# A one-layer streaming encoder on eight cores: from a hand-ordered kernel to an operation graph list-scheduled over three overlapped token tiles

## The chip, the cores and the metric

The kernel runs on all 8 cores of one Trainium2 chip: two dies of four cores. Every core does the same work on 4 of the 32 sequences. The time is device microseconds (us) of the slowest core. Engines are named as in the profile: PE is TensorE, PEld its weight loads, DVE is VectorE, ACT is ScalarE, POOL is GpSimd, SP is the queue that issues the DMAs. PSUM is the memory into which PE writes, used by both kernels as eight banks (`ps` of eight after; `psA` of six and `psT` of two before); an eviction is the DVE or ACT operation that reads a bank out.

The 8-core runs show two states. In the fast one the cores of a kernel agree within 1% (one run of before, 1.2%); in the slow one cores of one die, or of both, show a lower granted TensorE clock. **Only fast runs are compared below** unless a sentence says otherwise.

## The reference, cut to what matters

```python
D_MODEL = 1024; BATCH = 32; SEQ = 2048; DEPTH = 1; CHUNK = 64; D_FF = 4096; PLE_DIM = 256
def reference(x, p, ...):
    h = rmsnorm(x, g_mix)
    q, k, v, g, u, sv = split(h @ w_in)                  # 6 x 512 columns
    r = layernorm_nogain(chunk_retention(rotary(q), rotary(k) * 128**-0.5, v)) * ret_norm_g
    y_ret = silu(g) * r                                  # retention, 4 heads of 128
    y_sg = spatial_gating(gelu(u), gelu(sv), w_s, b_s, sg_norm_g)
    x = x + concat([y_ret, y_sg]) @ w_out                # "mixer"
    x = x + square(relu(rmsnorm(x, g_ffn) @ w_ff1)) @ w_ff2      # "FFN"
    x = x + sigmoid(rmsnorm(x, g_ple) @ w_ple_gate) * (p @ w_ple)   # "gate"
    return rmsnorm(x, g_final)
```

Inputs and output are float32; both kernels multiply in bfloat16. A core has 8192 tokens, worked through in 16 tiles of 512. Only the retention state ties one tile to the next.

## The kernel before

A small helper records operations per engine in the order in which the Python calls them, and works out semaphore waits. Each engine's program is its list, in that order. Per tile the order is written by hand: four 128-token blocks (`b`) are staggered by one or two steps in the mixer, then comes the FFN, then the gate.

```python
def norm_elem(b, xs_):                         # every norm: square-sum, rstd, scale
    S.add("act", ... activation(out=xsb[:, b, :], in_=xb[:, xs_, :], func=AF.Square, accum_out=stats...))
    rstd_from_ss(...)                          # DVE (mult, add), ACT Sqrt, DVE reciprocal
    S.add("act", ... activation(out=xsb[:, b, :], in_=xb[:, xs_, :], func=AF.Identity, scale=rstd))

def norm_transpose(b, gcol):                   # 8 PE transposes, then DVE eviction with the gain
    for kc in range(8): S.add("pe", ... transpose(out=psT[...], in_=xsb[:, b, ...]))
    S.add("dve", ... tensor_tensor(out=actT[...], in0=psT[...], in1=gT[...], op=ALU.mult))
# [cut]
norm_transpose(0, 0); norm_transpose(1, 0); stage_X1(0); stage_X1(1)
norm_transpose(2, 0); norm_transpose(3, 0); phase_B()
order = [("X2", 0), ("X2", 1), ("Y", 0), ("X", 2), ("Y", 1), ("Z", 0), ("X", 3), ("Y", 2), ("Z", 1),
         ("W", 0), ("Y", 3), ("Z", 2), ("W", 1), ("DT", 0), ("Z", 3), ("W", 2), ("DT", 1), ("W", 3),
         ("DT", 2), ("DT", 3)]
for nm, b in order: fns[nm](b)

for u in range(8):                             # FFN, first half: weights stream through a ring of 3
    slot = next_unit()
    for f4 in range(4):
        f = u * 4 + f4
        # 8 matmuls 128x512 into one PSUM bank
        S.add("act", ... Relu: psA -> scr)
        S.add("dve" if f % 2 == 0 else "pool", ... square: scr -> hT)
# [cut] second half: 32 matmuls into each of 4 banks, then a DVE add into the residual
# [cut] gate: norm_transpose, 8+2 matmuls, ACT Sigmoid, DVE multiply, POOL add, final norm, store
```

Activations use Silu, Gelu_apprx_tanh, Sigmoid and Sqrt. `w_in`'s v, g, u and sv columns, `w_out` and `w_ple_gate` stay in SBUF; q, k and the FFN weights stream. The float32 weights are cast to bfloat16 by DMAs on the POOL queue at the start.

Of the kernel before, what the change touches and what calls it, by code (L numbers as in the profile page):

```python
# [6 lines left out]
F32 = mybir.dt.float32  # L7
BF16 = mybir.dt.bfloat16
I32 = mybir.dt.int32
# [8 lines left out]
NRING = 3  # L18
N_CORES = 8
SEQ_PER_CORE = 4  # L20

class Op:
    __slots__ = ("eng", "fn", "dma", "ndma", "key", "val", "marked", "waits", "clock", "rank")

class Sched:
    ENGS = ("pe", "act", "dve", "pool", "sp")

    def __init__(self):
        self.eng_ops = {e: [] for e in self.ENGS}
        self.comp_ops = {e: [] for e in self.ENGS}  # L30
        self.issue_clock = {e: {} for e in self.ENGS}
        self.last_writer = {}
        self.readers = {}
        self.dma_cum = {}
        self.n_ops = 0

    def add(self, eng, fn, reads=(), writes=(), dma=None, ndma=1):
        op = Op()
        op.eng, op.fn, op.dma, op.ndma = eng, fn, dma, ndma
        op.marked = False  # L40
        self.eng_ops[eng].append(op)
        self.n_ops += 1
        if dma is None:
            self.comp_ops[eng].append(op)
            op.key, op.val = eng, len(self.comp_ops[eng])
        else:
            cum = self.dma_cum.get(dma, 0) + 16 * ndma
            self.dma_cum[dma] = cum
            op.key, op.val = ("dma", dma), cum
        deps = []  # L50
        for b in reads:
            w = self.last_writer.get(b)
            if w is not None:
                deps.append((w, 0))
        for b in writes:
            w = self.last_writer.get(b)
            if w is not None:
                deps.append((w, 1))
            for r in self.readers.get(b, {}).values():
                deps.append((r, 2))  # L60
        clk = self.issue_clock[eng]
        waits = {}
        for d, kind in deps:
            if d is op:
                continue
            if d.dma is None and d.eng == eng and dma is None:
                if eng == "pe" or kind != 0:
                    continue
# [8 lines left out]
        op.waits = list(waits.items())  # L77
        op.clock = dict(clk)
        op.clock[op.key] = op.val
        for b in reads:  # L80
            self.readers.setdefault(b, {})[op.key] = op
        for b in writes:
            self.last_writer[b] = op
            self.readers[b] = {}
        return op
# [9 lines left out]
def _emit_engine(eng_name, eobj, sched, sems):  # L95
    comp = sched.comp_ops
    for op in sched.eng_ops[eng_name]:
# [6 lines left out]
        if op.dma is not None:  # L104
            if not isinstance(ins, (list, tuple)):
                ins = [ins]
            assert len(ins) == op.ndma
            for i_ in ins:
                i_.then_inc(sems[op.key], 16)
        elif op.marked:  # L110
            ins.then_inc(sems[op.key], 1)

def _host_consts():
# [5 lines left out]
    ci = (t // 64)[:, None]  # L119
# [23 lines left out]
    ROT = np.zeros((SEQ // TT, 128, 2, TT), f32)  # L143
    for tp in range(SEQ // TT):
# [7 lines left out]

def build(nseq):
    NT = nseq * (SEQ // TT)
    NTOK = NT * TT
    nc = bass.Bass("TRN2", target_bir_lowering=False)
# [5 lines left out]
    p_d = din("p", [NTOK, 256])  # L162
    w_in_d = din("w_in", [D, 3072])
    w_out_d = din("w_out", [D, D])
    w1_d = din("w_ff1", [D, 4096])
    w2_d = din("w_ff2", [4096, D])
    wg_d = din("w_gate", [D, D])
    wple_d = din("w_ple", [256, D])
# [10 lines left out]
    ROT_d = din("ROT", [SEQ // TT, 128, 2, TT])  # L179
    IDENT_d = din("IDENT", [128, 128])  # L180
    out_d = nc.dram_tensor("out", [NTOK, D], F32, kind="ExternalOutput").ap()
    wqkb_d = nc.dram_tensor("wqkb", [2, 128, 4096], BF16, kind="Internal").ap()
    w1b_d = nc.dram_tensor("w1b", [8, 128, 4096], BF16, kind="Internal").ap()
    w2b_d = nc.dram_tensor("w2b", [8, 128, 4096], BF16, kind="Internal").ap()

    S = Sched()
# [5 lines left out]
    with es:  # L192
        win = sb("win", [128, 8, 2048], BF16)
        wout = sb("wout", [128, 8, 1024], BF16)
        wgs = sb("wgs", [128, 8, 1024], BF16)
        wple = sb("wple", [128, 2, 1024], BF16)
        ring = sb("ring", [128, NRING, 8, 512], BF16)
        xb = sb("xb", [128, 6, D], F32)
        actT = sb("actT", [128, 8, TT], BF16)
        big = sb("big", [128, 16384], BF16)  # L200
        rot = sb("rot", [128, 2, TT], F32)
        pbf = sb("pbf", [128, NB, 256], BF16)
        pT = sb("pT", [128, 2, TT], BF16)
        scr = sb("scr", [128, 4, 1024], F32)
        xsb = sb("xsb", [128, NB, D], BF16)
        Sst = sb("Sst", [128, 512], F32)
        Sbf = sb("Sbf", [128, 2, 512], BF16)
# [3 lines left out]
        retg = sb("retg_s", [128, 512], F32)  # L211
        sgg = sb("sgg_s", [128, 512], F32)
        bsT = sb("bsT_s", [128, 4], F32)
        wsTf = sb("wsTf", [128, 512], F32)
# [4 lines left out]
        MASKT = sb("MASKT_s", [128, 128], F32)  # L219
        stats = sb("stats", [128, 96], F32)  # L220
        st6 = sb("st6", [128, 2, 4, 6], F32)
        mv4 = sb("mv4", [128, 2, 4, 2], F32)
        psA = es.enter_context(nc.psum_tensor("psA", [128, 6, 512], F32))
        psT = es.enter_context(nc.psum_tensor("psT", [128, 2, 1024], BF16))

        hT = big[:, :].rearrange("p (f n) -> p f n", n=TT)
        qk = big[:, 0:4096].rearrange("p (c n) -> p c n", n=TT)
        OV = 4096

        def ov_bf(off, n):  # L230
            return big[:, OV + off: OV + off + n]

        def ov_f32(off, n):
            return big[:, OV + off: OV + off + 2 * n].bitcast(F32)

        PBSZ = 5120
        v_bf = [ov_bf(pb * PBSZ + 0, 512) for pb in range(2)]
        svn_bf = [ov_bf(pb * PBSZ + 512, 512) for pb in range(2)]
        ktok = [ov_bf(pb * PBSZ + 1024, 512) for pb in range(2)]
        PT = [ov_bf(pb * PBSZ + 1536, 512) for pb in range(2)]  # L240
        ybf = [ov_bf(pb * PBSZ + 2048, 1024) for pb in range(2)]
        gsb = [ov_f32(pb * PBSZ + 3072, 512) for pb in range(2)]
        ugb = [ov_f32(pb * PBSZ + 4096, 512) for pb in range(2)]
        assert OV + 2 * PBSZ <= 16384

        state = {"bank": 0, "tb": 0, "scr": 0, "unit": 0}

        def bankA():
            b = state["bank"]
            state["bank"] = (b + 1) % 6  # L250
            return b

        def bankT():
            b = state["tb"]
            state["tb"] = (b + 1) % 2
            return b

        def scr_slot():
            s_ = state["scr"]
            state["scr"] = (s_ + 1) % 4  # L260
            return s_

        def ld(eng, dst, src, key, wkey):
            S.add(eng, lambda e, dst=dst, src=src: e.dma_start(out=dst, in_=src), writes=[wkey], dma=key)

        ld("sp", gT[:, :], gT_d[:, :], "c_gT", "gT")
        ld("sp", DTm[:, :], DTm_d[:, :], "c_DTm", "DTm")
        ld("sp", KD[:, :], KD_d[:, :], "c_KD", "KD")
        ld("sp", EPSQ[:, :], EPSQ_d[:, :], "c_EPSQ", "EPSQ")
        ld("sp", MASKT[:, :], MASKT_d[:, :], "c_MASKT", "MASKT")  # L270
        ld("sp", wsTf[:, :], wsT_d[:, :], "c_wsT", "wsTf")
        ld("sp", bsT[:, :], bsT_d[:, :], "c_bsT", "bsT")
        ld("sp", retg[:, :], retg_d[:, :], "c_retg", "retg")
        ld("sp", sgg[:, :], sgg_d[:, :], "c_sgg", "sgg")
        ld("sp", gfin[:, :], gfin_d[:, :], "c_gfin", "gfin")
        ld("pool", ident[:, :], IDENT_d[:, :], "c_ident", "ident")
        S.add("dve", lambda e: e.tensor_tensor(
            out=wsTb[:, :].rearrange("p (g i) -> p g i", g=4),
            in0=wsTf[:, :].rearrange("p (g i) -> p g i", g=4),
            in1=MASKT[:, None, :].to_broadcast([128, 4, 128]), op=ALU.mult),  # L280
            reads=["wsTf", "MASKT"], writes=["wsTb"])

        units = []
        for t in range(NT):
            units += [("qk", 0), ("qk", 1)]
            units += [("w1", u) for u in range(8)]
            units += [("w2", u) for u in range(8)]
        unit_src = {"qk": wqkb_d, "w1": w1b_d, "w2": w2b_d}

        def issue_unit(n):  # L290
            if n >= len(units):
                return
            kind, u = units[n]
            slot = n % NRING
            src = unit_src[kind][u].rearrange("p (kc n) -> p kc n", kc=8)
            S.add("sp", lambda e, slot=slot, src=src: e.dma_start(out=ring[:, slot, :, :], in_=src),
                  reads=[(kind + "b", u)], writes=[("ring", slot)], dma=("ring", slot))

        def next_unit():
            n = state["unit"]  # L300
            state["unit"] = n + 1
            issue_unit(n + NRING - 1)
            return n % NRING

# [522 lines left out]
```

## Time and profile before

| | before |
|---|---|
| median of 5 runs (range) | 4698.6 us (4696.1 to 4703.2) |
| PE busy, DVE, ACT, POOL | 73%, 33%, 34%, 20% |
| chain that ended last | PE 56, DVE 14, ACT 14, issue 10 |
| mean granted TensorE clock | 0.877 to 0.884 |
| period of one tile | about 282 us |

These are lines of the page of the kernel before. In part 2 each digit is the busy share of one fortieth of the span, in tenths; PEclk is the granted clock. In a line of part 5, the last figures are the engine's idle time just ahead of these instructions and the releaser that ended most of it.

```profile
span 4710.4 us, 49849 instructions; the slowest of 8 cores (4686.3 to 4710.4 us)
...
PE 3445.9 (73%) x16912; PEld 1638.9 (35%) x17232; DVE 1555.5 (33%) x3425; ACT 1580.2 (34%) x2461; POOL 945.7 (20%) x811
...
PE   2557686867859677696867858677696876868678
...
PEclk9767798988989888898988989888898988989889
...
PE 56%; DVE 14%; ACT 14%; issue 10%; POOL 3%; another core or an unknown queue 1%; DVEq 1%; ACTq 0%; POOLq 0%
```

No engine is full, and the PE digits swing between 5 and 9 from slice to slice. The next answer, stretches of core 6, shows the two halves of one tile. After the stretch and its length come busy us (and instructions) of PE, PEld, DVE, ACT and POOL, then the granted clock, the DMA share and GB/s.

```profile
2340.00:2380.00 40.00, 39.79 (x183) 18.16 (x186) 3.44 (x5) 0.87 (x2) 1.04 (x1) 1.00 0.44 158
2403.00:2566.00 163.00, 99.50 (x535) 49.91 (x544) 80.11 (x185) 72.90 (x110) 40.47 (x32) 0.81 0.14 49
```

In the FFN, PE is full at clock 1.00 and the other engines idle. In the gate and mixer, PE is busy for 99.5 of 163 us at a mean clock of 0.81, and nothing else is full either. The list of what PE waited for in that core's whole run (releaser; total us, times, longest) says why:

```profile
PE psT L388 <- ACT xsb L381: 301.8, 82, 30.4
PE psA L448 <- DVE actT L392: 144.1, 15, 9.9
PE psA L418 <- DVE actT L392: 133.7, 16, 8.4
PE psT L498 <- POOL big L434: 119.9, 63, 25.2
PE psT L596 <- POOL big L589: 116.8, 32, 5.0
PE psA L696 <- DVE actT L392: 108.6, 32, 5.9
```

Norm scale (L381), transpose, eviction (L392), matmul: a chain over ACT, PE and DVE, and for y (L589) over POOL, on which PE waits at every link. ACT also reloads its function tables 289 times; the groups of ACT show where:

```profile
L367 ACT ACT_TABLE_LOAD x112 | 143.7, 1283 | 52.6 <-DVE stats L481 30.1 <-DVE stats L371 22.0
L458 ACT ACT_TABLE_LOAD x64 | 82.1, 1283 | 68.8 <-POOL big L575 42.2 <-PE psA L448 26.4
L462 ACT ACT_TABLE_LOAD x64 | 82.1, 1283 | 98.0 <-PE psA L448 97.6
L708 ACT ACT_TABLE_LOAD x48 | 61.6, 1283 | 59.9 <-PE psA L696 59.3
```

### The profile page before, as it was taken

The numbers are of one execution on the slowest core, as the hardware profiler recorded it, in microseconds if no ns is written. First come the engines' busy times: TensorE is split into PE (matmuls) and PEld (weight loads), VectorE is DVE, ScalarE is ACT, GpSimd is POOL, SyncE is SP. The second block draws the span as 40 slices with busy tenths as digits, with TensorE's granted clock in tenths as the row PEclk, the third lists the DMA queues.
The fourth block names the chain that finished last, engine by engine and source line by source line (L and its number), as shares of the span: only waits on it lengthen the run. The fifth ranks groups of instructions, "written<-read, shape, count | busy, mean of one in ns | idle before, by whom it ended". The sixth has DMA issues, their size and how long they took to land.

```text
span 4710.4 us, 49849 instructions; the slowest of 8 cores (4686.3 to 4710.4 us)
## 1 busy us (share of the span) xinstructions
PE 3445.9 (73%) x16912; PEld 1638.9 (35%) x17232; DVE 1555.5 (33%) x3425; ACT 1580.2 (34%) x2461; POOL 945.7 (20%) x811
## 2 busy tenths in 40 slices
PE   2557686867859677696867858677696876868678
PEld 1223343333424233343333434233343333434333
DVE  1402514224151432514225152332514325142342
ACT  1213324243242433324343242433314343242432
POOL 1210212212121221212212121221212212121121
PEclk9767798988989888898988989888898988989889
DMA  9963031221313213131221313213131221312212
GB/s 170 123 124 98 23 136 67 92 90 52 116 59 119 85 56 110 38 137 67 83 99 43 116 67 110 80 63 110 45 136 67 81 101 37 122 67 101 75 52 97
DMA packets 94601, 414.38 MB, mean 88 GB/s; under 512 B 8336, under 2 KB 35088, under 8 KB 57488
## 3 DMA queue, kind: packets, MB, share of 16 engines
q1 hardware_dynamic: 63648, 379.17, 22.8%
q0 software_dynamic: 30704, 32.02, 5.8%
q8 instruction: 141, 2.31, 0.2%
q14 instruction: 108, 0.88, 0.1%
HBM read 409.62 MB, written 52.43 MB: 98 GB/s over the span
## 4 chain that ended last, share of the span: by engine, by line
PE 56%; DVE 14%; ACT 14%; issue 10%; POOL 3%; another core or an unknown queue 1%; DVEq 1%; ACTq 0%; POOLq 0%
PE psA L643 19%; PE psA L678 19%; PE psA L448 7%; PE psA L696 3%; PE psA L418 3%; PE psA L611 3%; ACT L367 2%; ACT xsb L381 2%; ACT xsb L376 2%; DVE actT L392 2%; DVE scr L570 1%; ACT scr L723 1%; ACT stats L367 1%; DVE Sst L549 1%; DVE scr L431 1%
## 5 line engine op out<-in xcount | busy, mean ns | idle before, releaser
L643 PE MATMUL psA<-actT,ring 128*128 128x512 bf16 x4016 | 920.4, 390 | 27.9 <-DVE actT L392 23.6
L678 PE MATMUL psA<-ring,big 128*128 128x512 bf16 x4016 | 894.2, 383 | 4.4
L448 PE MATMUL psA<-win,actT 128*128 128x512 bf16 x1985 | 490.6, 406 | 277.5 <-DVE actT L392 144.1
L643 PEld LDWEIGHTS psA<-actT,ring 128*128 128x128 bf16 x4096 | 406.9, 100 | 530.5 <-issue 86.5
L678 PEld LDWEIGHTS psA<-ring,big 128*128 128x128 bf16 x4096 | 403.6, 99 | 492.4 <-issue 39.4
L376 ACT ACTIVATE xsb<-xb 128x1024 bf16<-128x1024 f32 x192 | 201.6, 1050 | 1027.3 <-DVE xb L683 814.2
L649 ACT ACTIVATE scr<-psA 128x512 f32<-128x512 f32 x512 | 305.8, 597 | 674.5 <-PE psA L643 657.6
L652 POOL TENSOR_TENSOR big<-scr 128x512 bf16<-128x512 f32 x256 | 265.8, 1038 | 974.4 <-ACT scr L649 974.4
L652 DVE TENSOR_TENSOR big<-scr 128x512 bf16<-128x512 f32 x256 | 177.2, 692 | 824.1 <-ACT scr L649 824.1
L713 POOL TENSOR_TENSOR xb<-xb,scr 128x512 f32<-128x512 f32 x128 | 162.0, 1266 | 1352.8 <-DVE scr L710 1342.9
L448 PEld LDWEIGHTS psA<-win,actT 128*128 128x128 bf16 x2048 | 207.9, 104 | 545.8 <-issue 351.9
L683 DVE TENSOR_TENSOR xb<-xb,psA 128x512 f32<-128x512 f32 x128 | 87.9, 687 | 823.5 <-PE psA L678 823.5
L388 PE MATMUL psT<-ident,xsb 128*128 128x128 bf16 x1536 | 136.5, 244 | 301.8 <-ACT xsb L381 301.8
L418 PE MATMUL psA<-actT,ring 128*128 128x512 bf16 x1007 | 247.1, 408 | 134.8 <-DVE actT L392 133.7
L696 PE MATMUL psA<-wgs,actT 128*128 128x512 bf16 x992 | 261.6, 411 | 109.5 <-DVE actT L392 108.6
L611 PE MATMUL psA<-wout,actT 128*128 128x512 bf16 x976 | 287.2, 453 | 4.0 <-issue 2.0
L553 ACT ACTIVATE Sbf<-Sst 128x512 bf16<-128x512 f32 x60 | 37.8, 630 | 622.6 <-DVE Sst L549 481.2
L381 ACT ACTIVATE xsb<-xb,stats 128x1024 bf16<-128x1024 f32 x192 | 220.3, 1148 | 70.3 <-DVE stats L368 70.3
L392 DVE TENSOR_TENSOR actT<-psT,gT_s 128x1024 bf16<-128x1024 bf16 x192 | 230.2, 1220 | 21.2 <-PE psT L388 20.9
L388 PEld LDWEIGHTS psT<-ident,xsb 128*128 128x128 bf16 x1536 | 111.2, 109 | 348.4 <-issue 330.0
L434 POOL TENSOR_TENSOR big<-scr 128x512 bf16<-128x512 f32 x128 | 162.2, 1268 | 194.7 <-DVE scr L431 194.7
L418 PEld LDWEIGHTS psA<-actT,ring 128*128 128x128 bf16 x1024 | 104.8, 103 | 271.9 <-issue 169.0
(75 smaller groups left out, 3126.0 us busy)
## 6 DMA issues: line engine op xcount, KB each, us to landing
ring<-w1b SPq DMA_DIRECT2D x128, 1024.0 KB, 5.0
ring<-w2b SPq DMA_DIRECT2D x128, 1024.0 KB, 4.8
xb<-x SPq DMA_DIRECT2D x64, 512.0 KB, 5.1
ring<-wqkb SPq DMA_DIRECT2D x32, 1024.0 KB, 4.8
out<-scr SPq DMA_DIRECT2D x64, 512.0 KB, 2.9
w1b<-w_ff POOLq DMA_DIRECT2D x8, 1024.0 KB, 142.6
rot<-ROT SPq DMA_DIRECT2D x16, 512.0 KB, 3.7
w2b<-w_ff POOLq DMA_DIRECT2D x8, 1024.0 KB, 198.3
```

The costliest lines, as they stand in the source:

```text
L376: S.add("act", lambda e: e.activation(out=xsb[:, b, :], in_=xb[:, xs_, :], func=AF.Square, accum_out=stats[:, b:b + 1]), reads=[("x", xs_) ...
L381: S.add("act", lambda e: e.activation(out=xsb[:, b, :], in_=xb[:, xs_, :], func=AF.Identity, scale=stats[:, 4 + b:5 + b]), reads=[("x", xs ...
L388: S.add("pe", lambda e, kc=kc: e.transpose(out=psT[:, tb, kc * 128:(kc + 1) * 128], in_=xsb[:, b, kc * 128:(kc + 1) * 128], identity=ident ...
L392: S.add("dve", lambda e: e.tensor_tensor(out=actT[:, :, b * 128:(b + 1) * 128], in0=psT[:, tb, :].rearrange("p (k n) -> p k n", k=8), in1= ...
L418: S.add("pe", lambda e, kc=kc, c4=c4, slot=slot, bk=bk: e.matmul(psA[:, bk, :], ring[:, slot, kc, c4 * 128:(c4 + 1) * 128], actT[:, kc, :] ...
L448: S.add("pe", lambda e, kc=kc, gi=gi, bk=bk: e.matmul(psA[:, bk, :], actT[:, kc, cols], win[:, kc, gi * 512:(gi + 1) * 512], start=(kc == ...
L611: S.add("pe", lambda e, kc=kc, bk=bk, hsl=hsl: e.matmul(psA[:, bk, :], actT[:, kc, cols], wout[:, kc, hsl], start=(kc == 0), stop=(kc == 7 ...
L643: S.add("pe", lambda e, kc=kc, f4=f4, slot=slot, bk=bk: e.matmul(psA[:, bk, :], ring[:, slot, kc, f4 * 128:(f4 + 1) * 128], actT[:, kc, :] ...
L649: S.add("act", lambda e, bk=bk, r_=r_: e.activation(out=r_, in_=psA[:, bk, :], func=AF.Relu), reads=[("psA", bk)], writes=[("scr", sl)])
L652: lambda e, f=f, r_=r_: e.tensor_tensor(out=hT[:, f, :], in0=r_, in1=r_, op=ALU.mult),
L678: S.add("pe", lambda e, f=f, fc=fc, slot=slot, fbk=fb[b], cols=cols: e.matmul(psA[:, fbk, :], hT[:, f, cols], ring[:, slot, fc, :], start= ...
L696: S.add("pe", lambda e, kc=kc, bg=bg, hsl=hsl: e.matmul(psA[:, bg, :], actT[:, kc, cols], wgs[:, kc, hsl], start=(kc == 0), stop=(kc == 7) ...
```

## The change

The intent: work on three tiles at once (mixer of tile t+1, FFN of t, gate of t-1), so that the mixer's chain runs behind FFN matmuls, and let a program choose the order.

- **Operation graph and list scheduler.** Every operation is a node with its buffers, a duration per engine it may run on, and a priority `vt` (the time at which a steady pipeline of 196 us per tile would want it). A greedy simulation on the host, at build time, gives each engine that comes free the ready operation of lowest `vt`. Its sequence becomes the engine's fixed program (experiment 2 shows PE idle with a matmul that could run behind the waiting one). Buffers come from pools. An *ordered* pool hands out slots only in priority order; a *free* pool (PSUM, the transposed tiles `TG`, statistics `st`) to whoever is ready first.
- **Streamed weights.** All 26 weight units of 1 MB (bfloat16) stream through two rings of three slots. At first use a unit is loaded as float32, cast and scaled by its gain on DVE or ACT, and written back for later tiles.
- **Deferred norms.** The host supplies transposed x and p. The projections run on unscaled data, and rstd is applied in the evictions. In the FFN only 1/ms remains, in the second half's eviction (scaling the input of relu squared by a factor scales its output by the square of it).
- **One set of functions.** Silu and sigmoid are written with tanh; rstd is a POOL power of -0.5 instead of Sqrt and reciprocal.
- The FFN runs in two halves, so `hT` needs 16 slots and 8 more evictions occur per tile.

```diff
-class Sched:                       # operations run in the order of the calls
-    ...
+KN_NSLOT = dict(ringM=3, ringF=3, TG=3, x=8, hT=16, qk=8, v=4, svn=2, ktok=2, PT=2, y=6, xsb=2, pT=1, stage=4,
+                rot=1, rel=3, gt=2, scr=10, st=16, psum=8, Sbf=2)
+for name, n in KN_NSLOT.items():
+    g.pool(name, n, ordered=name not in ("psum", "TG", "st"))
+def list_schedule(g):              # [cut to its core]
+    while n_left:
+        now = heapq.heappop(events)
+        for e in ("sp", "pe", "act", "dve", "pool"):
+            while free_at[e] <= now + 1e-9:
+                # of e's candidates by (vt, idx): the first that is ready and whose buffers can be had
+                op.start = now; free_at[e] = now + op.alts[e]
+                ...
+def mixer(t): vt = [(t - 1) * TILE]   # [bodies cut]
+def ffn(t):   vt = [t * TILE]
+def gate(t):  vt = [(t + 1) * TILE]
+for t in range(NT):
+    mixer(t); ffn(t); gate(t)
+order = list_schedule(g)
 # [cut]
-S.add("act", ... activation(out=y_ap, in_=a_ap, func=AF.Sqrt))
-S.add("dve", ... reciprocal(out=y_ap, in_=y_ap))
+g.add({"pool": (1.0, ... tensor_tensor(out=rstd, in0=ms, in1=NEGH, op=ALU.pow))})
-S.add("act", ... activation(out=gsb[pb], in_=psA[...], func=AF.Silu))
+g.add({"act": ( ... activation(out=ap(gs), in_=ps(p), func=AF.Tanh, scale=rsh1(b)))})
+g.add({"dve": ( ... scalar_tensor_tensor(out=ap(gs), in0=ap(gs), scalar=1.0, in1=ps(p), op0=ALU.add, op1=ALU.mult))})
-S.add("dve" if f % 2 == 0 else "pool", ... tensor_tensor(out=hT[:, f, :], in0=r_, in1=r_, op=ALU.mult))
+g.add({"dve": (0.69, fsq), "pool": (1.04, fsq)}, ...)      # the scheduler picks the engine
```

## The prediction

> **What bounds the kernel now.** The groups view counts 848 large (128x512) matmuls per 512-token tile (512 FFN, 192 input, 64 output, 80 gate) and about 200 small ones. In the table of stretches a dense FFN stretch (2340 to 2380 us, cores 4 to 7) holds 187 matmuls per 40 us, about 215 ns each, at granted clock 1.00, the other engines almost idle. A tile recurs every ~282 us: ~113 us FFN at that rate, then ~165 us (2403 to 2566 us: PE busy 99.5, DVE 80, ACT 73, POOL 40, clock 0.81) in which no engine is full. There the chain of waits alternates PE, DVE, ACT, POOL (PE waits 302 us for the normalised tile, 144 and 134 us for its evictions). Clock records fall to half in the gaps (~1100 us per core). So: a dependency-bound half and a TensorE-bound half, in series. The prologue wastes ~200 of its 290 us on casting DMAs.
>
> **What the change does.**
> Removes: transposes for the first norm and p (host), norm scaling before matmuls (moved into evictions), Sqrt/reciprocal pairs, most of 289 table loads x 1.28 us.
> Adds: x casts and extra loads, POOL power for rstd, 8 more FFN evictions (0.69 us).
> Moves: all weights stream: ~35 MB per tile with activations, against ~23. At ~200 us per tile that is ~175 GB/s; dense FFN took 158 GB/s at share 0.44, so it should fit.
> Overlaps: mixer(t+1), FFN(t), gate(t-1), so the serial chain hides behind FFN matmuls.
>
> Per tile, with durations of the trace: PE 848 x 0.216 + ~192 x 0.056 = 194 us at full clock; DVE ~105, ACT 65-85, POOL ~65. TensorE is the only limit: 16 x 194 = 3100 us. Nearly all that goes lies on the critical path: the 165 us stage shrinks to its PE work (~80 us).
>
> Losses (estimates): start 130-200 us (16 MB fp32 for mixer(0), then 32 MB plus write-back for FFN(0)); tail ~25 us; in-order stalls, PSUM slots, late weights 4 to 7%. Sum at full clock ~3450 to 3500.
>
> **The clock is the open term.** On cores 4 to 7 it is 0.8125[...] (matmuls ~265 ns), when all cores began the first FFN together. [...] later FFN stages, all cores dense for ~110 us, show 1.00. [...] I give ~60% that a die spends much of the run at 0.81. Entirely there: 16 x 239 + losses = ~4050.
>
> **Predicted: 3700 us, 8 in 10 within 3400 to 4100. Faster by over 2%: 0.96; within 2%: 0.02; slower: 0.02.**
>
> **What would show it.** PE nine tenths in most slices; half-clock records nearly gone; DVE about 50%, ACT and POOL 35-45%; DMA ~170 GB/s, share ~0.5; tile period ~200 us (clock 1.00) or ~245 us (0.81); chain of waits over 85% PE; low PE for the first 250-400 us, waiting for weight staging.
>
> **What would make it wrong.** PE waiting for ring slots (one issue queue blocked by an earlier wait); POOL power much dearer than 1 us, or DVE and POOL blocking each other[...]; a fixed order that stalls in-order PE by over 10%; the clock state.

The sum: ~3450 to 3500 us at full clock, ~4050 with all of it at 0.81, and 3700 between them by the ~60%. Readings of before: 40 us at 0.8125 hold 151 matmuls on core 6 (345 to 385 us; 263 ns each); of the first 290 us PE is busy 103 there, at a DMA share of 1.01, and the casting DMAs of the FFN weights land after 143 and 198 us (medians).

## The result, and the profile after

| | before | after |
|---|---|---|
| median of 5 runs | 4698.6 us | 3315.4 us |
| fast runs | all 5 | 3312.4, 3312.6, 3315.4 |
| slow runs | none | 3838.6 (one die at about 0.84), 3728.7 (both, 0.87 and 0.89) |
| ratio of fast runs, 95% interval | | 0.705 (0.704 to 0.706) |
| PE busy, DVE, ACT, POOL | 73, 33, 34, 20% | 94, 57, 35, 20% |
| mean clock (fast) | 0.877 to 0.884 | 0.981 to 0.987 |
| HBM read | 410 MB | 584 MB |

A ratio here is the mean time of one kernel's fast runs over the mean of the other's fast runs in the same group of runs, so it is not quite the ratio of the medians quoted. The new kernel is about 30% faster. The prediction of 3700 us, with 3400 to 4100, was too slow.

The same lines of the page, for the kernel after:

```profile
span 3310.8 us, 48382 instructions; the slowest of 8 cores (3299.4 to 3310.8 us)
...
PE 3121.7 (94%) x16270; PEld 1503.4 (45%) x16592; DVE 1898.4 (57%) x3842; ACT 1143.4 (35%) x1792; POOL 660.0 (20%) x605
...
PE   3697699999999999999999999999999999999998
...
PEclk9798899999999999999999999999999999999999
DMA  8888985564635546464564646446474555645442
...
PE 90%; DMA 4%; DVE 2%; issue 2%; ACT 1%; SPq 1%; POOL 0%; DVEq 0%; ACTq 0%; POOLq 0%
```

From the sixth slice to the last but one PE is at 9. (322 of its 16592 matmuls are missing from this core's records, so 94% is a little low.) Stretches of core 4, whose records are complete:

```profile
0.00:400.00 400.00, 275.60 (x1322) 124.87 (x1323) 173.02 (x406) 170.47 (x240) 74.49 (x69) 0.87 0.86 263
400.00:3200.00 2800.00, 2769.80 (x14784) 1333.40 (x14783) 1679.11 (x3370) 941.92 (x1504) 577.62 (x526) 1.00 0.55 189
3200.00:3312.00 112.00, 100.18 (x488) 46.21 (x486) 45.75 (x66) 30.69 (x49) 9.49 (x10) 0.97 0.31 114
```

Between 400 and 3200 us PE is busy 98.9% of the time at clock 1.00. What PE waited for in that stretch:

```profile
PE ps L617 <- ACT rel L1020: 9.3, 14, 0.7
PE ps L925 <- DVE TG L873: 8.8, 13, 0.7
PE ps L617 <- ACT scr L916: 8.5, 12, 0.7
PE ps L617 <- DVE scr L855: 2.9, 1, 2.9
```

That is 30 us in 2800, against more than 900 us in the six waits shown of before. One table load is left, at the start; Tanh, Gelu_apprx_tanh, Relu, Square and Copy all ran with no second one:

```profile
L669 ACT ACT_TABLE_LOAD x1 | 1.3, 1283 | 7.0 <-DMA stage<-xT 7.0
```

**Where the 3312 us are** (an estimate from the stretches above). In the middle a matmul takes 2769.80/14784 = 0.1873 us on average (large and small ones mixed). All 16592 at that rate are 3109 us. The first 400 us and the tail hold 124 + 12 us of idle PE and about 37 us by which their matmuls ran slower than that rate, at reduced clock. The middle lost 30 us. The sum is 3312. Per tile that is 16592/16 x 0.1873 = 194 us, the figure of the prediction. Of the 1385 us saved, some 300 are busy time of PE (3446 us before, 3146 on core 4 of after) at nearly the same number of matmuls; over the same change the half-clock records fell from about 1100 to about 100 us per core. The rest was idle time of PE.

### The profile page after: what moved, and what is told of

The parts are those of the page before. It is cut to its first block, busy times and chain, and to the rows that moved or that the text cites. A ratio compares the mean times of both kernels' runs of the same rounds, so it can differ in the third digit from the quotient of the medians.

```text
span 3310.8 us, 48382 instructions; the slowest of 8 cores (3299.4 to 3310.8 us)
## 1 busy us (share of the span) xinstructions
PE 3121.7 (94%) x16270; PEld 1503.4 (45%) x16592; DVE 1898.4 (57%) x3842; ACT 1143.4 (35%) x1792; POOL 660.0 (20%) x605
## 4 chain that ended last, share of the span: by engine, by line
PE 90%; DMA 4%; DVE 2%; issue 2%; ACT 1%; SPq 1%; POOL 0%; DVEq 0%; ACTq 0%; POOLq 0%
PE ps L617 85%; DMA stage<-wf 3%; PE ps L625 3%; DMA stage<-xT 1%; SPq L503 1%; PE ps L925 0%; PE ps L757 0%; PE ps L793 0%; PE ps L805 0%; PE ps L795 0%; ACT ringF L584 0%; ACT rel L1020 0%; DMA stage<-pT 0%; ACT scr L916 0%; DVE TG L873 0%
## 5 line engine op out<-in xcount | busy, mean ns | idle before, releaser
L617 PE MATMUL ps<-ringM,TG 128*128 128x512 bf16 x3996 | 955.1, 381 | 23.8 <-ACT rel L1020 8.7
L617 PE MATMUL ps<-TG,ringF 128*128 128x512 bf16 x4007 | 938.5, 380 | 25.3 <-ACT scr L916 8.5
L617 PE MATMUL ps<-ringF,hT 128*128 128x512 bf16 x3996 | 918.5, 382 | 44.8 <-ACT ringF L584 35.9
L1023 DVE TENSOR_TENSOR hT<-rel 128x512 bf16<-128x512 f32 x486 | 403.3, 830 | 408.7 <-ACT rel L1020 404.7
L617 PEld LDWEIGHTS ps<-ringF,hT 128*128 128x128 bf16 x4096 | 395.8, 98 | 493.4 <-issue 54.7
L617 PEld LDWEIGHTS ps<-TG,ringF 128*128 128x128 bf16 x4096 | 396.7, 98 | 487.3 <-issue 31.5
L617 PEld LDWEIGHTS ps<-ringM,TG 128*128 128x128 bf16 x4096 | 396.7, 98 | 480.2 <-issue 30.9
L1020 ACT ACTIVATE rel<-ps 128x512 f32<-128x512 f32 x512 | 304.5, 595 | 692.8 <-PE ps L617 686.9
L1040 DVE SCALAR_TENSOR_TENSOR xb<-ps,st,xb 128x512 f32<-128x512 f32 x256 | 191.0, 748 | 410.0 <-PE ps L617 409.7
L617 PE MATMUL ps<-TG,ringM 128*128 128x512 bf16 x991 | 243.9, 388 | 59.9 <-ACT ringM L573 53.9
```

The source lines that it names most:

```text
L617: r = e.matmul(out(), lhs(k), rhs(k), start=(start + k == 0), stop=(start + k == total - 1))
L1020: g.add({"act": (t_act(512), lambda e, p=p, r=r: e.activation(out=ap(r), in_=ps(p), func=AF.Relu))}, [(p, 0)], [(r, 0)], vt[0])
L1023: fsq = lambda e, r=r, o=o: e.tensor_tensor(out=ap(o), in0=ap(r), in1=ap(r), op=ALU.mult)
L1040: g.add({"dve": (0.69, lambda e, b=b, xx=xx, hsl=hsl, fbb=fb[b]: e.scalar_tensor_tensor(out=ap(xx)[:, hsl], in0=ps(fbb), scalar=stc(s4, 8 ...
```

## The experiments

Two theories at first. **A, overlap**: the time came from running the mixer's and gate's chain behind another tile's FFN; take that away and most of the gain goes. **B, cheaper work**: fewer operations in the chain (deferred norms, host transposes) and no table loads gave it. Later came **C, filling**: the scheduler's freedom to put any ready matmul, of any tile, into a hole. All kernels below give the right result. Unless said otherwise, each group ran on one chip with the kernel before beside it, at 4696 to 4705 us in the fast state (a run of 4751 and one of 4712 apart), so fast times may be set beside each other across groups to about 0.2%.

### 1. One tile at a time

Priorities in series (mixer, FFN, gate of a tile, then the next tile), and every input-projection matmul waits for the last gate matmul of the tile before it. The scheduler then found no order with the free PSUM pool (host-side deadlock), so this kernel's PSUM banks are handed out in priority order. **That is a second change**: as every PE operation opens its bank in that order, PE's order becomes fixed, and a matmul that is not ready holds up all behind it.

```diff
# serial_barrier (cut: three early loads moved forward)
-        g.pool(name, n, ordered=name not in ("psum", "TG", "st"))
+        g.pool(name, n, ordered=name not in ("TG", "st"))
-            vt = [(t - 1) * TILE]              # mixer
+            vt = [(t - 1) * 470.0]
-            vt = [t * TILE]                    # ffn
+            vt = [(t - 1) * 470.0 + 170.0]
-            vt = [(t + 1) * TILE]              # gate
+            vt = [(t - 1) * 470.0 + 375.0]
-    ... UB(u) + A1, [(p, 0)], vt[0])
+    ... UB(u) + A1 + after_gate(t), [(p, 0)], vt[0])
```

> The new kernel's operations, but a tile's input projection may only start after the last gate matmul of the tile before, so nothing but loads overlaps. Theory A (the gain is the overlap of three tiles): a tile takes the dense FFN, about 112 us, plus a mixer and gate chain of 110 to 150 us, so 3900 to 4400 us in all, TensorE idle near 30%. Rival B (the gain is the removed work: transposes, table loads, norm scaling): at most 3500 us. More idle gaps in TensorE, so if the slow state comes from never pausing, no slow run here.

Measured: 4425.0, 4426.0, 4419.8 us (and 4751.0 slow); ratio to before 0.941 (0.939 to 0.942). PE's two largest waits on core 0:

```profile
PE ps L625 <- POOL y L865: 476.9, 64, 8.1
PE ps L625 <- DVE xsb L996: 138.2, 81, 2.1
...
```

And the busy line of its page:

```profile
PE 3409.9 (77%) x16592; PEld 1590.7 (36%) x16592; DVE 1838.5 (42%) x3782; ACT 1238.5 (28%) x1892; POOL 623.3 (14%) x565
```

The chain is back: the transposes of y wait up to 8 us, 64 times, four per tile. PE also *works* longer, 3410 us instead of some 3146 (core 4 of after, complete), as the clock's mean falls to 0.90. So the cheaper operations (with the streaming and the new start) in this order are worth only 4699 - 4425 = 274 us; the other 1110 us came with the order. Theory B is out as the main term by itself. No run has the old operations (norms before the matmuls, transposes on PE) in the new order, so what the cheaper operations are worth there was not tested, except for the functions (4). And two things were undone here.

### 2. Only the fixed order

```diff
# plain_interleave: after, and
-        g.pool(name, n, ordered=name not in ("psum", "TG", "st"))
+        g.pool(name, n, ordered=name not in ("TG", "st"))
```

> The same operations and priorities, but PSUM banks are given out strictly in order of priority, so TensorE's groups run in a fixed interleave of the three tiles instead of in the order of modelled availability. Theory A1 (interleaving three tiles is enough): within 2% of the new kernel's fast runs, 3380 us at most. Theory A2 (filling each TensorE slot by the model is what keeps it 99% busy): TensorE idle 5% or more from 400 to 3000 us, 3450 to 3800 us.

Measured: 3865.2, 3866.1 (slow: 4274.6, 4057.4); ratio 0.823 (0.821 to 0.824). That is slower than either of its expectations allowed (3380 at most, or 3450 to 3800). PE's waits on core 0:

```profile
PE ps L625 <- POOL y L860: 348.3, 64, 8.0
PE ps L625 <- DVE y L934: 97.8, 48, 2.4
```

Three tiles overlap here, their priorities interleave as in the change, and still each y transpose makes PE wait. Interleaving alone does not hide the chain: at the moment of the wait, the FFN matmul that could run is *behind* the transpose in PE's program (at 1499.78 us on core 0 PE ends an idle gap of 3.69 us with the y transposes, and FFN matmuls follow at once). Hence theory C.

### 3. Filling without overlap

To separate the two, the barrier with a free PSUM pool. It needed a tie to avoid the deadlock: the two `w_ple` matmuls of a gate step come after that step's gate matmuls. `TG` is ordered (see 6).

```diff
# serial_greedy: serial_barrier, but
-        g.pool(name, n, ordered=name not in ("TG", "st"))
+        g.pool(name, n, ordered=name not in ("psum", "st"))
-                          [(pt, 0), c("wple0"), c("wple1")], [(p2, 0)], vt[0])
+                          [(pt, 0), (p, 0), c("wple0"), c("wple1")], [(p2, 0)], vt[0])
# serial_prio_greedy: the same without after_gate(t), so with serial priorities alone
```

> serial_barrier (4420 us) with PSUM banks given out by modelled availability as in the new kernel, barrier between tiles kept. If overlap is the main term and needs the fill to work: about 112 us FFN plus 125 to 145 us mixer and gate a tile, 4000 to 4350 us. If filling within one tile does most of it: 3700 us or less.

> The same without the barrier: a tile's own work has priority over the next tile's, which fills TensorE where it idles. If any overlap that the scheduler can find suffices: within 5% of the new kernel, 3313 to 3480 us. If the next tile's mixer must be spread over the whole FFN, as the new kernel's priorities do: 3600 us or more, since buffers let the next tile run only a little ahead.

Measured: serial_greedy 3602.2, 3599.2, 3618.9, 3615.6 (slow: 4099.3); serial_prio_greedy 3604.5, 3602.6, 3605.6 (slow: 3692.3). All seven runs of before on this chip were slow (4939 to 4980), so there is no ratio; the times are set beside those of the other groups. Of its two expectations serial_greedy met the second, filling within one tile (3700 or less), and is far from the first (4000 to 4350); serial_prio_greedy fell on the side on which overlap by priority brings nothing. The busy line on the page of serial_greedy:

```profile
PE 3249.2 (90%) x16592; PEld 1529.3 (42%) x16592; DVE 1857.9 (52%) x3805; ACT 1132.7 (31%) x1808; POOL 685.2 (19%) x626
```

Its two largest waits of PE, on core 0:

```profile
PE ps L617 <- ACT ringM L573: 62.0, 5, 38.3
PE ps L617 <- ACT TG L1004: 33.3, 30, 1.3
```

With only one tile on PE, POOL's y is out of the list (27.5 us are left for DVE's half of y). Within a tile, the projections of q, k, v, g, sv and u (192 large matmuls), the output projection's first blocks and other blocks' small matmuls are enough to fill most holes, if the order is chosen by what is ready. Taking the barrier away brought nothing: the two kernels' lists of waits agree to within about 3 us, and PE's records name the same tiles and shapes in the same order, all 16273 of core 0. So with serial priorities the scheduler had filled from the same tile anyway. The four kernels together (fast times, us):

| PE's order | one tile at a time | three tiles overlapped |
|---|---|---|
| fixed by priority | 4425 (serial_barrier) | 3866 (plain_interleave) |
| by what is ready | 3599 to 3619 (serial_greedy) | 3278 (ordered_tiles, as serial_greedy has its `TG` ordered; after: 3312) |

Filling is worth about 815 us without overlap and 550 to 590 with it; overlap is worth about 560 us in fixed order and 330 when filled. The two replace each other in part. Taken first, filling brings the larger piece by far (815 of 1145); taken second, about half. The entries differ by the `TG` and `w_ple` edits as well, so these figures are good to some tens of us.

### 4. The functions and their table loads

`old_functions` is after with Silu, Sigmoid and Sqrt with reciprocal in place of the tanh forms and the power. `serial_old_functions` has that and the edits of serial_barrier.

```diff
-            g.add({"pool": (1.0, lambda e: e.tensor_tensor(out=stc(st, 8, 4), in0=stc(st, 4, 4), in1=NEGH[:, 0:4],
-                                                          op=ALU.pow))},
+            g.add({"act": (0.2, lambda e: e.activation(out=stc(st, 8, 4), in_=stc(st, 4, 4), func=AF.Sqrt))},
+            g.add({"dve": (TINY, lambda e: e.reciprocal(out=stc(st, 8, 4), in_=stc(st, 8, 4)))},
# [cut: four more such; Silu for the g eviction; Sigmoid in the gate; the factors 0.5 become 1.0]
```

> The new kernel with its overlap, but with Silu, Sigmoid, Sqrt plus reciprocal as in the old one. ScalarE gets 300 to 500 table loads of 1.28 us (400 to 640 us on 1140 us busy, of 3315). Theory A: ScalarE has slack and the loads hide: within 2% of 3315 us, at most 3380. Rival B (functions matter by themselves): 3500 us or more.

> The same without overlap, and Silu, Sigmoid, Sqrt plus reciprocal in place of the Tanh forms and the POOL power. Theory A: the table loads (over 250 of 1.28 us) lie on the serial chain, so 100 to 300 us longer than serial_barrier, near the old kernel. Rival B: even more, 300 us or over.

Measured: old_functions 3443.4, 3447.5 (slow: 3630.9, 3850.9), ratio 0.733 (0.731 to 0.734); serial_old_functions 4577.5, 4574.0, 4573.3 (slow: 4647.4), ratio 0.973. The functions are worth 131 us in the new kernel and 151 in the serial one. The first lies between what was expected: 3380 at most if the loads hide, 3500 or more if not. The page of old_functions:

```profile
PE 3168.2 (92%) x16592; PEld 1501.7 (44%) x16592; DVE 1842.8 (54%) x3922; ACT 1705.8 (50%) x2431; POOL 505.3 (15%) x382
...
PE 75%; ACT 8%; issue 5%; DMA 5%; DVE 4%; POOL 1%; SPq 0%; DVEq 0%; ACTq 0%; POOLq 0%
```

ACT now does 401 table loads of 1.283 us, 514 us in all. ACT gets 8% of the chain. Overlap does not make this swap free: ACT has half its time to spare, and still the kernel lost as much as a quarter of the loads' time. The host's model knows nothing of the loads, so it plans ACT's results too early. That this is the cause was not tested: the swap changes operations of DVE and POOL as well, and a model wrong by half in all three engines cost only 20 us (5).

The reverse, the new functions in the kernel before, took two tries:

```diff
# before_one_table2: before, and (cut)
-            S.add("act", lambda e: e.activation(out=y_ap, in_=a_ap, func=AF.Sqrt), reads=keys, writes=keys)
-            S.add("dve", lambda e: e.reciprocal(out=y_ap, in_=y_ap), reads=keys, writes=keys)
+            S.add("pool", lambda e: e.tensor_tensor(out=y_ap, in0=a_ap, in1=NEGH[:, 0:k], op=ALU.pow), ...)
# and in the helper, for every operation (waits on earlier ones of the same engine)
-                if eng == "pe" or kind != 0:
+                if eng == "pe" or kind == 2:
# tanh forms for Silu and Sigmoid; the halving of w_ple and ret_norm_g once, in tile 0
# before_one_table: the same, with both halvings at the start
```

> The old kernel with Tanh forms and the POOL power alone, nothing overlapped: table loads go from 289 to about 1. Theory A: under a fifth of the gain, 4450 to 4650 us, because only the loads on the chain count and the POOL power costs about 1 us where Sqrt and reciprocal cost 0.37. Rival B: 4300 us or less.

> before_one_table mended: its two scalings of constants sat early in the in-order queues of GpSimd and ScalarE and held the first norms back by about 250 us. Now they are issued just before their first use. Theory: the functions alone are worth little in the old serial kernel, since POOL power plus its waits costs as much on the chain as Sqrt, its table load and the reciprocal: 4600 to 4720 us. Rival: 4550 or less, as serial_old_functions minus serial_barrier (152 us) suggests.

Measured: before_one_table 4937.8, 4936.8, 4937.0 (slow: 5047.8), ratio 1.050. It was flawed: the halving of `w_ple` stood early in POOL's program, ahead of the norms' powers, and PE's first instruction came at 281 us. before_one_table2 mends that: 4793.3, 4798.3 (slow: 4971, 5075, 4964), ratio 1.021 (1.019 to 1.023). Also missed: with one table load left, the old kernel became **2% slower**. But this kernel has **a second edit**, the helper's: an operation now also waits for an earlier one of its own engine that wrote the same buffer (the kernel after has this rule too). Lines of before, and under the dots the same of before_one_table2. The waits are those of the whole run on the slowest core; the last line of each is on core 0:

```profile
PE psA L448 <- DVE scr L570: 49.7, 16, 3.4
PE psA L540 <- DVE scr L570: 24.9, 12, 2.4
1623.11 1.37 DVE L570 TENSOR_SCALAR scr<-psA,mv,stats 128x128 f32<-128x128 f32 x4
...
PE psT L391 <- ACT xsb L384: 414.7, 96, 131.7
PE psA L451 <- DVE scr L576: 104.4, 32, 5.4
PE psA L546 <- DVE scr L576: 57.5, 12, 4.8
1656.33 1.96 DVE L576 TENSOR_SCALAR scr<-psA,mv,stats 128x128 f32<-128x128 f32 x4 [1.27 <-POOL stats L370]
```

The wait for the norms was 301.8 us before, but 131.7 of the 414.7 us are one wait at the start, and it is made good: the second half of the first FFN starts at 323 us, against 328 before (core 0). Over the 15 tiles from there on, the norms' waits are 271 us against 262. What grew is the wait for DVE's scaling of the retention output (`scr`). On core 0 its four operations take 1.96 us instead of 1.37 per block, as each now waits for the one before; with the two groups of four statistics ahead of them (1.50 and 1.04 us instead of 0.89 and 0.38) that is 1.9 us more. The hop to POOL for the power makes the same chain 0.6 us longer (1.27 us instead of 0.69 from the variance to the scaling; medians). So most of what this chain lost came with the helper's edit, and **the 2% are not shown to be the price of the functions**: no run has them in the old kernel without that edit. What is shown is a gain of 130 to 150 us in the kernels whose order was planned with them.

### 5. Is the schedule fragile?

The prediction feared that a fixed order worked out from modelled durations would stall an in-order PE by 4 to 7%, or over 10%. So: a wrong model, fewer buffers, and both.

```diff
# wrong_durations: elementwise durations of the model times 1.5 (PE and DMA unchanged)
-        op.alts = {e: d for e, (d, f) in alts.items()}
+        op.alts = {e: d * (1.5 if e in ("act", "dve", "pool") else 1.0) for e, (d, f) in alts.items()}
# tight_buffers:  y=6 -> 4, stage=4 -> 3, rel=3 -> 2, scr=10 -> 7
# tight_wrong:    both
```

> The order is made by the same scheduler, which now believes that every VectorE, ScalarE and GpSimd operation takes 1.5 times as long as it does. If the accuracy of the modelled times keeps the stalls near 1%, this costs 3% or more (over 3410 us). If the buffers absorb differences between the model and the chip, it stays within 1.5% (3365 us at most).

> Right durations, small buffers (7 scratch, 4 y, 2 relu, 3 staging slots). If slack is what keeps TensorE at 99%: 3370 us or more, near tight_wrong (3383). If the right model is enough: after 400 us still 98.5% or more; the third staging slot less costs the start 20 to 40 us, so 3335 to 3360 us.

> wrong_durations (elementwise operations believed 1.5 times as long) with smaller buffers: 7 scratch tiles for 10, 4 y for 6, 2 relu for 3, 3 staging slots for 4. If the slack of the buffers absorbed the wrong model, less slack shows it: over 3400 us, TensorE idle 3% or more from 500 to 3000 us. If not, within 1% of wrong_durations (3335 us).

Measured: wrong_durations 3335.3, 3324.1, 3344.4 (slow: 3398.1), ratio 0.710; tight_buffers 3349.8, 3346.5, 3348.6 (slow: 3556.0), ratio 0.711; tight_wrong 3383.2, 3382.7 (slow: 3965.5, 3558.8), ratio 0.720. Against 3312 us: +0.7%, +1.1%, +2.1%. Core 4 of tight_buffers:

```profile
0.00:400.00 400.00, 261.18 (x1276) 120.30 (x1276) 172.59 (x407) 161.37 (x230) 74.10 (x69) 0.89 0.83 246
400.00:3150.00 2750.00, 2702.20 (x14420) 1300.59 (x14421) 1649.37 (x3321) 922.76 (x1465) 571.65 (x520) 1.00 0.55 191
```

Fewer buffers cost both at the start (one staging slot fewer, 246 GB/s instead of 263) and later (98.3% busy; of the 48 us idle there 25 are two waits for weights being staged). tight_wrong fell between its two expectations. Even with the model off by half and tight buffers the loss stays near 2%. In these runs the order's exact times matter little. The feared term was too large.

### 6. The three stalls of each tile

The waits of 0.7 us in the list of after occur about once per tile each. `TG` has three slots in a free pool, so two tiles' transposed inputs can be handed out in an unlucky order.

```diff
# ordered_tiles: after, and
-        g.pool(name, n, ordered=name not in ("psum", "TG", "st"))
+        g.pool(name, n, ordered=name not in ("psum", "st"))
```

> The three transposed-tile buffers given out in order, nothing else. If this removes the small stalls after 400 us (3 of 0.7 us in a tile, 30 us in all): 3280 to 3290 us. If those went because of the fifth slot or by chance of the order: 3305 to 3325 us.

Measured: 3278.0, 3277.3, 3277.6, 3280.2 (slow: 3360.1, 3480.6), ratio 0.696. Core 4 from 400 to 3150 us:

```profile
400.00:3150.00 2750.00, 2749.09 (x14709) 1327.29 (x14708) 1682.54 (x3387) 899.88 (x1454) 582.05 (x536) 1.00 0.56 191
```

And all that PE still waits for in that stretch:

```profile
PE ps L617 <- ACT TG L874: 0.8, 1, 0.8
```

35 us gained, about as much as the stalls that went (30 us of waits). PE is now busy 99.97% of that stretch. A stricter allocation made a better schedule here, while for PSUM the stricter one cost 550 us: freedom is not good or bad by itself. That the order of hand-out causes the stalls is shown; by which chain of events is not.

### 7. The start

PE's first matmul comes at 40.6 us, as SP issues 4 MB of x before the first weights; then until 400 us the DMAs run at 263 GB/s with a share of 0.86.

```diff
# late_x: the residual loads of tiles 0 and 1 wait for the first k matmul
+                    [(START, 0)] if t < 2 else [], [(X[t, b], 0), (X[t, b], 1)],
# better_start: late_x, and w2's write-back only at its second use
# fifth_slot: ordered_tiles, stage=4 -> 5, scr=10 -> 8
# deep_stage: fifth_slot and late_x
```

> Two edits of the start alone: the first two tiles' loads of x for the residual wait until the first key matmuls, and the w2 units are written back as bf16 at their second use instead of their first. Theory: the first 400 us are bound by DMA bytes, so 4 MB less before the first matmul (about 15 us at 265 GB/s) and 8 MB less in the first FFN (about 28 us) give 15 to 45 us, 3270 to 3300 us in fast runs, steady state unchanged. Rival (the start is bound by casts or by dependencies): within 8 us of 3313.

> The later x loads alone. By better_start the first matmul comes 13 us earlier; if the start is bound by bytes, those 4 MB are loaded before 400 us all the same and the gain shrinks: 3298 to 3308 us. If the first matmul's time carries through: 3295 to 3302 us.

> Five staging slots, eight scratch tiles and ordered buffers, without the x loads' edit. Theory (four slots in flight limit the start): 3265 to 3285 us, first 400 us at 275 GB/s or more against 265. Rival (the x loads gave it all): 3300 us or more.

> The later x loads of better_start alone, and 5 staging slots of 512 KB for 4 (8 scratch tiles for 10; the three transposed-tile buffers given out in order, else the scheduler deadlocks). Theory: the first 400 us are limited by four slots of 512 KB in flight at about 8.1 us each, 259 GB/s, as measured; a fifth gives up to 25% more rate there: with the 13 us of the x loads 3270 to 3295 us. Rival (the DMA engines themselves are the limit, share 0.86): 3298 to 3306 us, only the x loads' gain.

Measured (fast):

| kernel | times, us | ratio to before |
|---|---|---|
| late_x | 3317.0, 3315.1, 3312.5, 3312.2, 3311.4, 3316.3 | 0.7035 |
| better_start | 3301.6, 3304.7, 3300.8, 3305.7 | 0.7032 |
| fifth_slot | 3266.9, 3270.5, 3275.2, 3271.3, 3267.8 | 0.6942 |
| deep_stage | 3263.1, 3264.4, 3267.2, 3260.3 | 0.6946 (0.6936 to 0.6956) |

late_x brought the first matmul to 27.2 us and gained nothing, against both of its expectations: by 400 us PE has done 1324 matmuls on core 4, against 1322 in after, with the DMAs at 264 and 263 GB/s. What PE did earlier it waited for later. better_start gained some 10 us, less than expected: the deferred work (w2 in float32 once more, and its 8 MB of write-back) came due in the second tile.

```profile
560.00:600.00 40.00, 28.20 (x134) 12.88 (x136) 8.00 (x11) 18.36 (x21) 0.00 (x0) 0.87 0.91 315
```

This is core 4 of better_start: PE 28 of 40 us busy, DMA share 0.91. fifth_slot, on the chip of ordered_tiles, gained 8 us over it: with five staging slots the DMAs of the first 400 us reached 279 GB/s.

```profile
0.00:400.00 400.00, 281.33 (x1423) 130.59 (x1424) 187.77 (x431) 180.58 (x255) 74.17 (x69) 0.91 0.92 279
```

ordered_tiles has 275.54 us of PE there, and 275 GB/s. **deep_stage is the fastest of all, 3264 us, 1.5% below the change.** It beat its expectation of 3270 to 3295, but that had not counted what ordered `TG` gives alone. Slow runs, left out of the table: late_x 3863.6; better_start 3623.9, 3482.2, 3735.5; fifth_slot 3396.5; deep_stage 3561.5. Whether its late x loads add to fifth_slot is not settled: the two ran on different chips. The start still has the DMAs near full (share 0.92 in fifth_slot): 52 MB of float32 weights come in, are cast, and 26 MB go back.

### 8. Is there room for the DMA traffic?

```diff
# more_traffic: with every ringF reload, a second copy of the 1 MB unit from DRAM to DRAM
+                    dma(lambda: junk_d[jb.slot], lambda: wb_d[u], [(wb_buf[name], 0)], [(jb, 0)], vt, ...)
# paced_traffic: 8 such copies per tile, each waiting for an FFN matmul of that tile
```

> For each streamed FFN weight unit, one more copy of 1 MB from DRAM to DRAM: 16 MB more read and 16 MB more written in each tile of 196 us, DMA share from 0.54 to about 0.8 or more. If streaming has headroom, as predicted, within 1% of 3313 us. If loads were close to late (ring waits), 3% or more and waits of TensorE for DMA.

> more_traffic mended: there nothing held the copies back, so all of them ran in the first 2000 us. Now a copy of 1 MB from DRAM to DRAM follows the first matmuls of each streamed w1 unit, 8 MB more read and 8 written in each tile; by what the copies cost in more_traffic (share 0.97 for 194 GB/s) the DMA share goes from 0.54 to about 0.75. If streaming has headroom: within 1% of 3313 us and no waits of TensorE for DMA. If not: 2% or more, waits on ring loads.

Measured: more_traffic 4516.1, 4507.4 (slow: 4955.6, 4634.1). It was flawed: nothing held the copies back, and they all ran in the first 2000 us at a DMA share of 0.95 to 0.99. It says nothing about the change. paced_traffic 3321.2, 3319.4 (slow: 3920.2, 3891.1, 3594.2; too few fast runs for a ratio), +0.2%. Core 0:

```profile
400.00:3150.00 2750.00, 2710.49 (x14465) 1303.41 (x14464) 1641.25 (x3313) 911.40 (x1455) 570.61 (x520) 1.00 0.72 231
```

With 231 GB/s instead of 190 and a share of 0.72, PE is 98.6% busy. After the start there is room for a fifth more traffic. That streaming itself costs nothing follows only in part: no run keeps the weights in SBUF.

### What could not be tried

For two slots per weight ring and for seven PSUM banks the scheduler found no order at all, so no such kernel was built; the least buffers that the change needs were not found by a run. No run sets the clock's state.

## Why the prediction was right or wrong

The direction, the limit and most of the parts were right; the time was 385 us too long, and the range missed.

- **"194 us per tile at full clock", "TensorE is the only limit": right.** 0.1873 us per matmul x 1037 per tile is 194 us; the chain is 90% PE; DVE took 60% and ACT 34% of the middle stretch.
- **Wrong, the first and largest step: "The clock is the open term ... ~60% that a die spends much of the run at 0.81".** It moved the estimate from about 3475 to 3700. In the profiled fast run all eight cores show a mean of 1.00 from 400 to 3200 us, with PE busy 98.9% of it (core 4); 0.8125 shows for only 7 to 15 us per core, around 168 to 187 us (on cores 0 and 1 also once or twice up to 435 us). The ~60% rested on the rule, which is not shown here. What the prediction had from the trace of before spoke against it: after the first FFN, stages with all cores dense show 1.00, and no core has 0.8125 after 462 us. It gave the rule more weight than the trace. (How long 0.8125 lasted there: the trace has 114 to 130 us on each core of that die, between 228 and 462 us.) Two of five runs were slow (3838.6 with one die at 0.84), so the state is real; 4050 "entirely there" was not seen. Slow runs of variants with a die at a mean of 0.81 to 0.83 took 3864 to 3965 (late_x, paced_traffic, tight_wrong). The draw of states has its part in the miss: with one more slow run of the five the median would have been the lowest slow time, 3729 us or less, and so most likely inside the range. It is not shown to come from density: over all groups, 19 of 57 runs of the dense overlapped kernels were slow, and 18 of 50 of the kernel before, whose PE is busy 73% (7 of the 18 on the one chip where no dense overlapped kernel ran). serial_barrier, PE busy 77%, had a slow run too, which its expectation excluded if never pausing were the cause. What trips it stays open. A prediction should have priced it as a share of slow runs, apart from the fast time.
- **Wrong, the term "in-order stalls, PSUM slots, late weights 4 to 7%"** (124 to 217 us): measured 30 us in the middle, 1.1%, and 1 us in ordered_tiles. Wrong durations and tight buffers together brought it to 2% (PE 98.0% busy from 500 to 3000 us on core 0 of tight_wrong, whose records are complete). Here a list schedule that fills by readiness left hardly any such term. Why it was put at 4 to 7% the prediction does not say.
- **"Start 130-200 us": right**, 124 us idle and about 28 at reduced clock. **"Tail ~25 us"**: 12 idle and about 9 at reduced clock.
- **"So the serial chain hides behind FFN matmuls": half right.** The chain is hidden, but not by the overlap alone. In fixed order the overlapped kernel still waited 348 us for y; chosen by readiness, even one tile alone filled most holes (3599 to 3619 us). What overlap adds to that is some 330 us. The prediction never named the filling as a term of its own, and my first theory A had to be given up in that form.
- **"Nearly all that goes lies on the critical path": right in sum, not for each part.** The cheaper operations alone gave 274 us of the 1385, in serial fixed order; the functions are 151 of them there, and 131 us in the new kernel. In the old kernel the swap lost 2%, but together with an edit of the helper.
- **DMA "~175 GB/s, share ~0.5", "should fit": right.** 189 GB/s, share 0.55; paced_traffic had room for 40 GB/s more.
- **"POOL 35-45%": wrong,** 20%. The scheduler gave 486 of the 512 FFN squares to DVE. That cost no time, since DVE was not the limit.
- **"POOL power much dearer than 1 us": did not occur.** 0.56 to 0.57 us for 128x1 and 1.02 to 1.39 us for 128x4 (means of its groups in after). **"DVE and POOL blocking each other": for DVE it occurs.** From the timelines of core 4 of after (start us, duration us, instruction):

```profile
1034.78 1.26 POOL L713 TENSOR_TENSOR qk<-scr 128x512 bf16<-128x512 f32 x1 [5.51 <-DVE scr L710]
...
1034.98 1.62 DVE L1023 TENSOR_TENSOR hT<-rel 128x512 bf16<-128x512 f32 x1 [0.34 <-ACT rel L1020]
```

POOL starts 0.20 us ahead of DVE and ends at 1036.04; DVE's square ends at 1036.60, after 1.62 us. Of the 486 such squares of this core, the 347 that no POOL operation overlaps take 0.68 to 0.69 us each; the 139 others average 1.17 us, 1.75 at most. Over the run the squares average 0.83 us. By what means a POOL operation holds DVE up is not shown, and whether DVE holds POOL up was not examined. The change can afford it: in ordered_tiles they average 0.80 us (core 4), and PE waits 0.8 us in all.

## What to carry to other kernels

When an in-order engine waits on a chain, ask first whether a ready instruction stands behind the waiting one in its program: choosing the order by readiness was worth at least as much here as overlapping tiles, and it made even a single tile fairly dense (PE 90%). Change one thing at a time: the swap of functions was a gain of 4% in the new kernel, but the loss of 2% in the old one came with a second edit, and the waits that grew lie for the most part with that edit. Price a clock state that some runs have and others lack as a share of runs, not as a mean, and where a rule and a trace differ, weight the trace.
